# Three sums of magnitudes instead of eight, three whole products and a new order, in a two-level seven-product matmul

## The chip, the cores and the metric

The kernel runs on one core of a Trainium2 chip. The metric is the device time of one execution in microseconds (us); lower is better. The core's engines are PE (matmuls; PEld is its weight loads), DVE and ACT (vector and scalar work), POOL (a second, slower vector engine) and SP (here only the queue that issues DMAs). Each engine works through its own queue in order.

## The reference

```python
B, S, D = 8, 2048, 2048          # x: [B, S, D], w: [D, D], float32
cs = np.cumsum(x, axis=1)
diff = cs - shifted(cs)          # shifted by one row: diff is x again
return np.matmul(diff, w)
```

So what must be computed is x @ w: 16384 rows, 2048 by 2048 weights.

## The kernel before, in words

The 128 row tiles of x (128 rows each) are worked in two ways. The first four ("plain") are multiplied directly while the weights arrive: per half h of the output columns and per 128 rows ko of the weights, `plain.h.r.ko` is two matmuls for row tile r. x reaches the kernel in quarters there (`first x.q.r`, 256 KB each), which DVE casts (`cast x`), PE transposes (`turn x`) and an engine copies out of PSUM (`turned x`). Weights come as 512 KB pieces (`w.h.ko`), cast to 16 bits by ACT (`cast w`).

The other 124 tiles go in 31 groups of four, numbered 0 to 30 (`period[0]`; `PERIOD` is one group in the order table). A group's four tiles g, h, k, l are a 2 by 2 block matrix, multiplied by seven products P1 to P7 instead of eight (Strassen's scheme in Winograd's form). P6 is done whole. Each of the other six is itself done by seven quarter products instead of eight (class `Seven`): a quarter product is four matmuls of 128x512. For these the weights of each product exist as sums too: of the quarters t11, t12, t21, t22 of a block, Q2 and Q3 (and for most Q4) are made once by DVE (`quarters`, `make`; Q2 overwrites t12's place) and Q1, Q3 or Q4 that aren't kept are made anew in each group into one buffer, `flow` (`ask`). T1 to T4 are sums of weight blocks, made once at the start. `Seven.slot(i)` records the sums of x that a quarter product needs on DVE (`s1` to `s4`), the matmuls (`P3.0` to `P3.6`), copies between PSUM banks or to a lent buffer on ACT (`first`, `out2`, `out4`), an addition on DVE (`middle`) and, after it, one on POOL (`last`). Results are put together in C11, C12, C21, C22 by ACT (`keep`), DVE and POOL, and SP writes them out (`put`).

x of the groups comes by `load` (512 KB) into one of three buffers of F, is cast by ACT (`narrow`), summed in magnitude by ACT as a check of its range (`weigh`), and turned by a DMA (`turn`); the next `load` into that buffer waits for `turn` and `weigh`. `see` is a like check on results: ACT sums the magnitudes of a whole C (128x1024), and its unneeded output goes into the spare half of the F buffer that was loaded last, so a later `load` into that buffer waits for it as well. All checks meet in `judge` (`flag1` to `flag9`, one 1x1 matmul, `vote`); if it finds a fault, the whole product is done again in a slow way, which doesn't happen with these inputs.

Nothing here is scheduled by the order of the code: every operation is recorded with a label, and `emit` sorts all of them by `places`, a table of numbers by label with rows for groups 0, 1, 2, 28, 29, 30 and one (`None`) for all others. Each engine's queue is its share of that sorted list. Every POOL operation also waits for the last DVE operation ahead of it in the list.

Of the kernel before, what the change touches and what calls it, by code (L numbers as in the profile page):

```python
# [10 lines left out]
def kernel(  # L11
# [6 lines left out]
    nc = tc.nc  # L18
# [12 lines left out]
    ALU = mybir.AluOpType  # L31
# [17 lines left out]
    const = ctx.enter_context(tc.tile_pool(name="const", bufs=1))  # L49
    Wall = const.tile([P, KH, 4 * NH], f32, name="W")  # L50
# [7 lines left out]
    seen_c = tiny[:, 8:16]  # L58
# [309 lines left out]
    class Right:  # L368
# [26 lines left out]
        def ask(self, name):  # L395
            if name in self.s:
                return self.s[name]
            p, q, op = {
                "Q1": ("t22", "Q2", SUB),
                "Q3": ("Q2", "t11", SUB),  # L400
                "Q4": ("t21", "Q2", SUB),
            }[name]
            tensor(f"{self.name}.{name}", flow, self.s[p], self.s[q], op)
            return flow
# [22 lines left out]
    in_3.quarters(early[3])  # L427
    in_7.quarters(late[0], late[1])
# [7 lines left out]
    for some, to in zip((in_3, in_5, in_1, in_2), late[3:]):  # L436
        some.make("Q4", "t21", "Q2", SUB, to)

# [23 lines left out]
    class Seven:  # L462
        def __init__(self, name, g, h, side, right, to, room, lent):
            self.name = name
            self.a11, self.a12 = (piece(g, side, n) for n in range(2))
            self.a21, self.a22 = (piece(h, side, n) for n in range(2))
            self.right = right
            (self.g0, self.g1), (self.h0, self.h1) = to
            self.r1, self.r2 = room or (self.a21, self.a11)
            self.r4 = self.r2 if room else self.a12  # L470
            self.lent = lent
# [3 lines left out]

        def slot(self, i):
            n = self.name
# [29 lines left out]
    def see(c, i):  # L507
        if period[0] == 1:
# [4 lines left out]
                lambda: nc.scalar.activation(other, c, ABS, accum_out=seen_c[:, i : i + 1]),  # L513
# [52 lines left out]
    def group(g, xy, zv):  # L566
        h, k, l = g + 1, g + 2, g + 3
# [3 lines left out]
        def ready(t, i):  # L571
            nonlocal ready_last
            ready_last = t, i
# [50 lines left out]
        for u, v, p, s, t in ((C21g, C22g, zv[0], "g", g), (C21h, C22h, zv[1], "h", h)):  # L624
            c = free.pop(0)
            for i in range(2):
                tensor(f"C12{s}.{i}", c[:, i, :], p[i], v[:, i, :], ADD)
                if s == "h" and i == 1:
                    plus("P3.last", c[:, i, :], lz, "pool")
# [12 lines left out]
        for c, v, p, s in ((C21g, C22g, xy[0], "g"), (C21h, C22h, xy[1], "h")):  # L642
            for i in range(2):
                plus(f"C21{s}+P7.{i}", c[:, i, :], p[i])
                if s == "h" and i == 1:
# [53 lines left out]
    def judge():  # L699
# [4 lines left out]
        dve("flag4", lambda: ins.tensor_scalar(flags[:, 8:16], seen_c, FINITE, None, ALU.is_le))  # L704
        dve("flag5", lambda: ins.tensor_reduce(flags[:, 1:2], flags[:, 8:16], AX.X, ALU.min))
# [36 lines left out]
            'first x.0.0': -710913, 'cast w.0.0': -708588, 'numbers turned': -640017,  # L742
            'eye': -620640, 'first x.0.1': -615478, 'first x.2.3': -611089,
# [517 lines left out]
```

## Time and profile before

| | us |
|---|---|
| median of 3 runs | 1457.49 (1455.3 to 1457.54) |
| profiled execution, its own time | 1456.21 |
| its span in the trace | 1454.3 |
| PE busy | 1424.5, 98% of the span |
| DVE / ACT / POOL busy | 1302.5 / 1046.1 / 552.1 |

The profiled execution's time is 1.9 us more than its span, and 1.3 us less than the median. PE is busy nearly always, so the time is PE's work plus the gaps in it; the gaps are few, and they lie at the start, in the first groups and in the last. Groups 3 to 27 take 43.6 us each.

### The profile page before, as it was taken

To read this page: it belongs to the slowest core of one execution; us is meant where nothing else is said; L and a number is where in the kernel's file an instruction comes from. 1 tells how busy PE (TensorE), PEld (TensorE's weight loads), DVE (VectorE), ACT (ScalarE), POOL (GpSimd) and SP (SyncE) were. 2 spreads that over 40 slices of the span, in tenths; PEclk is the share of its full clock that TensorE was granted. 3 is DMA by queue.
4 is the path that set the end of the run, shared out by engine and by line. 5 is a ranking of instruction groups with operands and counts; after the bars stand their busy time and mean duration, and the time that the engine had idled before them with its cause. 6 is when DMAs were issued, how large, how long until landed. Compare 5 with 4: busy or idle time off the path is not lost. (4 is left out here: it accounts for less than half of the span.)

```text
span 1454.3 us, 20618 instructions
## 1 busy us (share of the span) xinstructions
PE 1424.5 (98%) x6543; PEld 630.1 (43%) x6543; DVE 1302.5 (90%) x2107; ACT 1046.1 (72%) x1716; POOL 552.1 (38%) x376
## 2 busy tenths in 40 slices
PE   8999899999999999999999999999999999999997
PEld 3443334444444444444444444444444444444443
DVE  2799879999999999999999999999999999999997
ACT  5877867777777767777777777777777777776773
POOL 0014423444433444433444433444433444433444
PEclk9999999999999999999999999999999999999999
DMA  9998698888888898788888888898888898888883
GB/s 362 350 259 217 188 231 237 250 249 229 240 243 239 247 249 230 239 241 240 247 250 229 242 236 244 247 254 225 246 238 240 252 253 222 247 239 226 252 223 121
DMA packets 343792, 351.64 MB, mean 242 GB/s; under 512 B 270976, under 2 KB 270976, under 8 KB 343680
## 3 DMA queue, kind: packets, MB, share of 16 engines
q1 hardware_dynamic: 343680, 350.29, 84.3%
q8 instruction: 52, 0.85, 0.2%
q14 instruction: 60, 0.49, 0.1%
HBM read 150.99 MB, written 134.22 MB: 196 GB/s over the span
## 5 line engine op out<-in xcount | busy, mean ns | idle before, releaser
L126 POOL TENSOR_TENSOR arena<-arena 128x512 f32<-128x512 f32 x372 | 551.9, 1491 | 896.8 <-DVE arena L126 623.7
L129 ACT COPY arena<-b 128x512 f32<-128x512 f32 x729 | 407.2, 588 | 257.6 <-PE b L450 127.7
L450 PE MATMUL b<-W,x 128*128 128x512 f16 x2108 | 521.2, 379 | 2.1 <-DVE x L126 1.0
L450 PEld LDWEIGHTS <-x 128*128 128x128 f16 x3224 | 314.5, 98 | 396.4 <-issue 21.9
L126 DVE TENSOR_TENSOR arena<-W 128x2048 f16<-128x2048 f16 (+1 forms) x287 | 367.6, 1281 | 23.5 <-PE b L450 23.4
L450 PE MATMUL b<-W,arena 128*128 128x512 f16 x1364 | 344.0, 379 | 5.8 <-DVE arena L126 3.8
L450 PEld LDWEIGHTS <-arena 128*128 128x128 f16 x1984 | 189.1, 98 | 254.8 <-DVE arena L126 35.9
L129 ACT CAST F<-F 128x1024 f16<-128x1024 f32 x248 | 260.2, 1049 | 44.5 <-DMA F<-in_x_dram 40.6
L450 PE MATMUL b<-arena,x 128*128 128x512 f16 x1116 | 281.6, 379 | 4.4 <-ACT arena L129 4.4
L163 ACT ACTIVATE F<-F 128x1024 f16<-128x1024 f16 x248 | 263.1, 1062 | 1.1
L126 DVE TENSOR_TENSOR arena<-arena,b 128x512 f32<-128x512 f32 x372 | 247.7, 678 | 11.1 <-PE b L450 9.6
L543 PE MATMUL b<-W,x 128*128 128x512 f16 x992 | 250.1, 381 | 1.6 <-DVE x L126 1.6
L126 DVE TENSOR_TENSOR x<-x,x 128x1024 f16<-128x1024 f16 (+1 forms) x372 | 232.8, 633 | 6.2 <-DMA x<-F 3.8
L129 ACT COPY b<-b 128x512 f32<-128x512 f32 x186 | 107.3, 577 | 78.0 <-DVE arena L126 62.0
L450 PE MATMUL b<-arena 128*128 128x512 f16 x620 | 159.1, 379 | 2.3 <-DVE arena L126 2.1
L126 DVE TENSOR_TENSOR b<-b,arena 128x512 f32<-128x512 f32 x217 | 150.1, 692 | 11.4 <-ACT arena L129 11.0
L543 PEld LDWEIGHTS <-x 128*128 128x128 f16 x992 | 95.3, 98 | 122.3 <-DVE x L126 12.0
L126 DVE TENSOR_TENSOR arena<-b,arena 128x512 f32<-128x512 f32 x155 | 105.3, 681 | 18.5 <-PE b L450 17.0
L126 DVE TENSOR_TENSOR arena<-x,x 128x512 f16<-128x512 f16 x124 | 56.8, 458 | 31.9 <-PE b L450 31.7
L126 DVE TENSOR_TENSOR arena<-x 128x512 f16<-128x512 f16 x124 | 59.3, 479 | 1.2 <-PE b L450 0.2
L126 DVE TENSOR_TENSOR x<-x 128x512 f16<-128x512 f16 x124 | 56.6, 457 | 3.3 <-PE b L450 1.5
L126 DVE TENSOR_TENSOR arena<-arena,x 128x512 f16<-128x512 f16 x124 | 54.2, 437 | 2.6
(43 smaller groups left out, 301.4 us busy)
## 6 DMA issues: line engine op xcount, KB each, us to landing
F<-in_x_dram SPq DMA_DIRECT2D x248, 512.0 KB, 5.0
out_dram<-arena SPq DMA_DIRECT2D x240, 512.0 KB, 3.7
W<-in_w_dram SPq DMA_DIRECT2D x32, 512.0 KB, 9.0
out_dram<-arena SPq DMA_DIRECT2D x32, 256.0 KB, 3.4
W<-in_x_dram SPq DMA_DIRECT2D x16, 256.0 KB, 7.0
x<-F SPq DMA_TRANSPOSE x248, 3.2
```

What stands on the lines that cost most here:

```text
L126: record(label, engine, lambda: on.tensor_tensor(dst, p, q, op))
L129: record(label, "act", lambda: nc.scalar.copy(to, p))
L163: return nc.scalar.activation(other, data, ABS, accum_out=m)
L450: said = nc.tensor.matmul(to, a[:, ds(k * P, P)], b[:, k, :], start=(start and k == 0), stop=(k == 3), skip_group_check=True,)
L543: said = nc.tensor.matmul(to[n], half(t, 0)[:, k, :], T2[k][:, n, :], start=False, stop=(k == KH - 1), skip_group_check=True,)
```

## The change

It has four parts.

1. `see`: instead of all eight C of group 1, three are summed: `see.3` (C21h) of group 29, `see.1` (C11h) and `see.5` (C12h) of group 30. `flag4` and `flag5` work on three columns.
2. P3 and P7 in group 0 and P7 in group 30 are done whole, by eight quarter products (`w0` to `w7`) without sums of x or of weights. In group 30 the quarter t12 of in_7's block, which Q2 has overwritten by then, is made again (`in7.t12`).
3. The sums of quarters for in_3 and in_7 (six, `in3.make` and `in7.make`) are recorded in group 1 rather than in group 0.
4. All rows of `places` have new numbers.

```diff
+    FROM3, FROM7 = 1, 1
+    LAST = (END - PLAIN) // 4 - 1
...
-    seen_c = tiny[:, 8:16]
+    seen_c = tiny[:, 8:11]
...
+                "t12": ("t22", "Q3", SUB),
...
-    in_3.quarters(early[3])
-    in_7.quarters(late[0], late[1])
...
+    def by_quarters():
+        if period[0] == FROM7:
+            in_7.quarters(late[0], late[1])
+        if period[0] == FROM3:
+            in_3.quarters(early[3])
+            in_3.make("Q4", "t21", "Q2", SUB, late[3])
...
+            self.whole = (name == "P3" and period[0] < FROM3) or (
+                name == "P7" and (period[0] < FROM7 or period[0] == LAST)
+            )
...
+        def slot_whole(self, i):
+            pairs = [
+                (to, a, b, start)
+                for to, p, q, c in (
+                    (self.g0, self.a11, self.a12, 1),
+                    (self.g1, self.a11, self.a12, 2),
+                    (self.h0, self.a21, self.a22, 1),
+                    (self.h1, self.a21, self.a22, 2),
+                )
+                for a, b, start in ((p, f"t1{c}", True), (q, f"t2{c}", False))
+            ]
+            for j in (0, 1) if i == 0 else (i + 1,):
...
+                quarter(f"{self.name}.w{j}", to, a, self.asked[b], start)
...
     def see(c, i):
-        if period[0] == 1:
+        rows = {1: LAST, 5: LAST, 3: LAST - 1}
+        if i in rows and period[0] == rows[i]:
...
     def group(g, xy, zv):
+        by_quarters()
...
-                if s == "h" and i == 1:
+                if s == "h" and i == 1 and not P3.whole:
                     plus("P3.last", c[:, i, :], lz, "pool")
...
-            'P1.0': -29977, 'P1.s1': -20682, 'P1.s2': -16636, 'P1.first': -15550, 'P1.2': -15057,
+            'P1.0': -30279, 'P1.s1': -22233, 'P1.first': -16350, 'P1.s2': -16053, 'P1.2': -15126,
```

What the new numbers do to the queues is seen at three places.

**DVE, group 0, from the `middle` of P5 on, before** (b are PSUM banks, x the turned tiles, W the weight blocks, arena everything else). The rows are in turn P5.middle, in3.Q1, in4.make Q2, S3g, in7.make Q2, P3.s2, keep C22h.1, S3h, in3.make Q4, P3.middle, P3.s4 and C12g.0:

```order
L126 TENSOR_TENSOR b7_81<-b5_79,arena_70 128x512
L126 TENSOR_TENSOR arena_70<-W_58 128x2048
L126 TENSOR_TENSOR W_58<-arena_70,W_58 128x4x512
L126 TENSOR_TENSOR x20_66<-x21_67,x00_62 128x1024
L126 TENSOR_TENSOR W_58<-arena_70,W_58 128x4x512
L126 TENSOR_TENSOR x01_63<-x11_65,x01_63 128x512
L126 TENSOR_TENSOR arena_70<-b5_79,arena_70 128x512
L126 TENSOR_TENSOR x30_68<-x31_69,x10_64 128x1024
L126 TENSOR_TENSOR arena_70<-W_58 128x2048
L126 TENSOR_TENSOR b5_79<-b7_81,arena_70 128x512
L126 TENSOR_TENSOR x01_63<-x01_63 128x512
L126 TENSOR_TENSOR arena_70<-b4_78,arena_70 128x512
```

The same stretch now, from P5.middle: S3g, T3.7, keep C22h.1, S4h, in4.make Q2, in4.Q1, C12g.1, S3h, C12g.0, P4.s1 and then the first two of the moved sums, in3.make Q2 and in7.make Q3 of group 1:

```order
L128 TENSOR_TENSOR x20_66<-x21_67,x00_62 128x1024
L128 TENSOR_TENSOR W_58<-W_58 128x2x512
L128 TENSOR_TENSOR arena_70<-b5_79,arena_70 128x512
L128 TENSOR_TENSOR x11_65<-x11_65,x10_64 128x1024
L128 TENSOR_TENSOR W_58<-arena_70,W_58 128x4x512
L128 TENSOR_TENSOR arena_70<-W_58 128x2048
L128 TENSOR_TENSOR arena_70<-b5_79,arena_70 128x512
L128 TENSOR_TENSOR x30_68<-x31_69,x10_64 128x1024
L128 TENSOR_TENSOR arena_70<-b4_78,arena_70 128x512
L128 TENSOR_TENSOR x31_69<-x31_69 128x512
L128 TENSOR_TENSOR W_58<-W_58 128x4x512
L128 TENSOR_TENSOR arena_70<-W_58 128x2048
```

The sums for P3 are gone from between, and these two moved sums stand behind C12g.0, which uses P3's result. Of the other four, in3.make Q3 stands far ahead, before the first sum of x in group 0; in7.make Q2 and in3.make Q4 stand just ahead of P4.s4 of group 0, and in7.make Q4 inside group 1.

**ACT, where group 1 ends and group 2 begins, before.** The rows are P1.out2 of group 2, three `see` of group 1, P1.out4, P2.first, keep C11g.0 and .1, narrow7.0, P2.out2, narrow6.0 and keep C11h.0 (narrow and see belong to group 1):

```order
L129 COPY arena<-b_76 128x512
L513 ACTIVATE F,tiny<-arena 128x1024 x3
L129 COPY arena<-b_76 128x512
L129 COPY b_78<-b_80 128x512
L129 COPY arena<-b_74 128x512
L129 COPY arena<-b_75 128x512
L129 CAST F<-F 128x1024
L129 COPY arena<-b_80 128x512
L129 CAST F<-F 128x1024
L129 COPY arena<-b_76 128x512
```

Now no `see` stands there, and narrow6.0 (the first row) comes ahead of P1.out2, followed by narrow7.1, P1.out4, P2.first, keep C11g.1 and .0, and narrow7.0:

```order
L131 CAST F<-F 128x1024
L131 COPY arena<-b_76 128x512
L131 CAST F<-F 128x1024
L131 COPY arena<-b_76 128x512
L131 COPY b_78<-b_80 128x512
L131 COPY arena<-b_75 128x512
L131 COPY arena<-b_74 128x512
L131 CAST F<-F 128x1024
```

**ACT, where group 29 ends and group 30 begins, now.** The rows are P1.first of group 30, weigh5.1 and weigh6.1 of group 29, see.3, P1.out2, P2.first, P1.out4, narrow6.0 of group 29, keep C11g.0, narrow7.1 and P2.out2:

```order
L131 COPY b_74<-b_76 128x512
L165 ACTIVATE F,told<-F 128x1024 x2
L546 ACTIVATE F,tiny<-arena 128x1024
L131 COPY arena<-b_76 128x512
L131 COPY b_78<-b_80 128x512
L131 COPY arena<-b_76 128x512
L131 CAST F<-F 128x1024
L131 COPY arena<-b_74 128x512
L131 CAST F<-F 128x1024
L131 COPY arena<-b_80 128x512
```

Here a `see` has come in: see.3 stands behind P1.first, and in SP's queue load6.0 of group 29 stands behind it (its buffer is the one that see.3 writes to). Before, load6.0 of group 29 came ahead of P1.first of group 30.

More of the change, by code (lines that the diff above doesn't have):

```diff
@@ L435 @@
     in_4.make("Q2", "Q3", "t11", ADD, in_4.s.pop("t12"))
-    for some, to in zip((in_3, in_5, in_1, in_2), late[3:]):
+    for some, to in zip((in_5, in_1, in_2), late[4:]):
         some.make("Q4", "t21", "Q2", SUB, to)
+    def by_quarters():
[4 more added lines that the diff above has]
+            in_3.make("Q4", "t21", "Q2", SUB, late[3])
     room = [rooms_at[:, j, :] for j in range(2)]
@@ L467, in __init__ @@
             self.right = right
+            self.whole = (name == "P3" and period[0] < FROM3) or (
+                name == "P7" and (period[0] < FROM7 or period[0] == LAST)
+            )
+            self.asked = {}
             (self.g0, self.g1), (self.h0, self.h1) = to
@@ L474, in sum @@
             tensor(f"{self.name}.s{n}", to, p, q, op, engine)
+        def slot_whole(self, i):
[10 more added lines that the diff above has]
+            for j in (0, 1) if i == 0 else (i + 1,):
+                to, a, b, start = pairs[j]
+                if b not in self.asked:
+                    self.asked[b] = self.right.ask(b)
+                quarter(f"{self.name}.w{j}", to, a, self.asked[b], start)
         def slot(self, i):
+            if self.whole:
+                return self.slot_whole(i)
             n = self.name
@@ L512, in see @@
                 "act",
-                lambda: nc.scalar.activation(other, c, ABS, accum_out=seen_c[:, i : i + 1]),
+                lambda: nc.scalar.activation(other, c, ABS, accum_out=seen_c[:, i // 2 : i // 2 + 1]),
             )
@@ L572, in ready @@
             nonlocal ready_last
-            ready_last = t, i
+            if t < END:
+                ready_last = t, i
             load(t, i)
@@ L644, in group @@
                 plus(f"C21{s}+P7.{i}", c[:, i, :], p[i])
-                if s == "h" and i == 1:
+                if s == "h" and i == 1 and not P7.whole:
                     plus("P7.last", c[:, i, :], lx, "pool")
@@ L703, in judge @@
         dve("flag3", lambda: ins.tensor_reduce(flags[:, 0:1], fits, AX.XY, ALU.min))
-        dve("flag4", lambda: ins.tensor_scalar(flags[:, 8:16], seen_c, FINITE, None, ALU.is_le))
-        dve("flag5", lambda: ins.tensor_reduce(flags[:, 1:2], flags[:, 8:16], AX.X, ALU.min))
+        dve("flag4", lambda: ins.tensor_scalar(flags[:, 8:11], seen_c, FINITE, None, ALU.is_le))
+        dve("flag5", lambda: ins.tensor_reduce(flags[:, 1:2], flags[:, 8:11], AX.X, ALU.min))
         dve(
@@ L734 @@
         0: {
[7 rows of a table removed]
-            'first x.0.0': -710913, 'cast w.0.0': -708588, 'numbers turned': -640017,
-            'eye': -620640, 'first x.0.1': -615478, 'first x.2.3': -611089,
[156 rows of a table removed]
-        },
[47 rows of a table removed]
-        },
[46 rows of a table removed]
[6 rows of a table added]
+            'numbers': -1144010, 'first x.0.1': -1046174, 'numbers turned': -988555,
[56 rows of a table added]
+            'cast w.1.4': -249602, 'one': -249513, 'turn0.0': -249053, 'out': -248802,
[96 rows of a table added]
+        },
[48 rows of a table added]
+        },
[45 rows of a table added]
         },
         28: {
[44 rows of a table removed]
[44 rows of a table added]
         },
         29: {
[45 rows of a table removed]
[46 rows of a table added]
         },
         30: {
[43 rows of a table removed]
[42 rows of a table added]
         },
         None: {
[44 rows of a table removed]
[44 rows of a table added]
         },
```

853 rows, old and new, of the table places are left out of this document.

## Prediction

> **What bounds the kernel now.** I read the page first.
>
> ```profile
> span 1454.3 us, 20618 instructions
> PE 1424.5 (98%) x6543; PEld 630.1 (43%) x6543; DVE 1302.5 (90%) x2107; ACT 1046.1 (72%) x1716; POOL 552.1 (38%) x376
> ```
>
> PE is the bound, so time can come only from fewer matmuls or from the 30 us in which PE stands. To place those, I cut the span where a group's first product starts (from the timeline of PE); the columns are length, busy time of PE, PEld, DVE, ACT and POOL, granted clock, DMA share and GB/s.
>
> ```profile
> 0.00:10.42 10.42, 7.63 (x23) 2.73 (x23) 2.96 (x9) 3.27 (x3) 0.20 (x4) 1.00 0.80 258
> 10.42:46.02 35.60, 31.93 (x190) 15.77 (x191) 11.44 (x23) 27.09 (x30) 0.00 (x0) 1.00 1.03 406
> ...
> 72.36:119.63 47.27, 44.17 (x202) 19.16 (x201) 45.80 (x66) 34.94 (x60) 10.48 (x7) 1.00 0.92 252
> 119.63:165.80 46.17, 42.72 (x193) 18.31 (x192) 41.30 (x65) 35.73 (x60) 16.21 (x12) 1.00 0.73 205
> 165.80:214.65 48.85, 43.66 (x189) 18.46 (x188) 39.01 (x61) 35.12 (x61) 12.73 (x10) 0.97 0.85 217
> 214.65:1305.05 1090.40, 1089.48 (x5001) 483.13 (x5000) 1003.39 (x1625) 797.93 (x1326) 445.60 (x301) 1.00 0.85 241
> 1305.05:1397.85 92.80, 91.72 (x421) 40.66 (x420) 87.01 (x139) 65.31 (x109) 41.34 (x27) 1.00 0.87 235
> 1397.85:1447.12 49.27, 46.80 (x210) 19.93 (x208) 45.95 (x78) 24.54 (x42) 23.55 (x17) 1.00 0.49 155
> 1447.12:1454.29 7.17, 0.00 (x0) 0.00 (x0) 0.98 (x2) 0.00 (x0) 2.02 (x2) 0.74 0.54 191
> ```
>
> The rows are: the start in two pieces, groups 0, 1 and 2, groups 3 to 27, 28 and 29, 30, and the tail. Groups 3 to 27 have 0.9 us of idle PE in 1090.40: nothing is left there, and their 1090.40/5001 = 0.218 us is the price of a matmul. Groups 0, 1 and 2 have 3.1, 3.4 and 5.2 us, group 30 has 2.5, the tail 7.2. DVE is busy for 45.80 of group 0's 47.27 us: there it is DVE that paces. Whom PE waits for in those groups, from its timeline (start, length, and in brackets the idle time before and who ended it):
>
> ```profile
> 76.05 1.02 PE L450 MATMUL b<-W,arena 128*128 128x512 f16 x4 [1.37 <-ACT b L129]
> 103.86 1.04 PE L450 MATMUL b<-W,x 128*128 128x512 f16 x4 [0.51 <-DVE x L126]
> 114.41 1.04 PE L450 MATMUL b<-arena 128*128 128x512 f16 x4 [0.88 <-DVE arena L126]
> ...
> 128.00 1.90 PE L450 MATMUL b<-W,arena 128*128 128x512 f16 x8 [1.90 <-DVE arena L126]
> 149.24 1.89 PE L450 MATMUL b<-W,x 128*128 128x512 f16 x8 [0.77 <-ACT b L129]
> ...
> 175.35 1.90 PE L450 MATMUL b<-W,arena 128*128 128x512 f16 x8 [0.72 <-DVE arena L126]
> 185.94 1.02 PE L450 MATMUL b<-arena,x 128*128 128x512 f16 x4 [2.34 <-ACT arena L129]
> 187.37 3.40 PE L543 MATMUL b<-W,x 128*128 128x512 f16 x8 [0.40 <-DVE x L126]
> ```
>
> The last row is eight matmuls in 3.40 us, twice their usual time. The clock by stretches says why:
>
> ```profile
> 187.61:191.02 3.41, 3.41 (x10) 1.21 (x9) 3.38 (x7) 1.87 (x5) 0.00 (x0) 0.50 0.99 303
> 184.20:187.61 3.41, 1.26 (x6) 0.41 (x6) 1.68 (x4) 3.25 (x6) 0.00 (x0) 1.00 0.76 182
> ```
>
> After 3.41 us in which PE was busy for 1.26, the clock was granted by half for the next 3.41 us: 1.7 us lost on top of the waits. The Trainium skill ("TensorE: Matmul & The Clock Gate", Part 1) tells of windows of this length, but halves the clock after an idle one; here a wait of 2.34 us was enough.
>
> **Part 1, the sums of C.** The wait of 2.34 us is for a copy on ACT (P2.out4), and its chain is read on ACT and SP:
>
> ```profile
> 175.89 1.06 ACT L513 ACTIVATE F<-arena 128x1024 f16<-128x1024 f32 x1
> ...
> 183.61 1.04 ACT L129 CAST F<-F 128x1024 f16<-128x1024 f32 x1 [2.90 <-issue]
> 184.82 1.07 ACT L129 COPY arena<-b 128x512 f32<-128x512 f32 x2 [0.16 <-DMA out_dram<-arena]
> ```
>
> ```profile
> 177.07 0.33 SPq L145 DMA_DIRECT2D F<-in_x_dram  x1
> ```
>
> see.3 ends at 177.0, and at 177.07 the load goes out that needs the F buffer see.3 wrote to; narrow6.0 waits for it until 183.61, and the copy P2.out4 stands behind narrow6.0. Without the `see` of group 1 that load waits only for weigh5.1. So the 2.34 goes, and with it the half clock; eight sums also leave ACT in groups 1 and 2:
>
> ```profile
> L513 ACT ACTIVATE F<-arena 128x1024 f16<-128x1024 f32 x8 | 8.4, 1056 | 0.5 <-POOL arena L126 0.3
> L513 ACT ACTIVATION_READ_ACCUMULATOR F<-arena 128x1 f32 x8 | 1.5, 188 | 0.0
> ```
>
> That is 9.9 us of ACT. The same chain is built anew in group 30: see.3 of group 29 waits for POOL's P4.last, load6.0 for see.3, narrow6.0 for the load, and P2.out2 stands behind narrow6.0, with P2.4 behind that. Counted in products from the end of P4.6 of group 29 (0): see.3 runs from about 1.1 to 2.4 (POOL has three operations of 1.49 to do behind P7.6, which ends 3.5 us before), the load lands 5.0 later, at 7.4, then come narrow6.0 (1.05), keep C11g.0 (0.6), narrow7.1 (1.05) and P2.out2 (0.6): 10.7. P2.4 is due nine products of 0.87 after P4.6 and a short wait, at 8.1. That is a wait of 2.6, an estimate from the two rows below; with a load faster or slower by 1 it is 1.6 to 3.6. I take 2.4.
>
> ```profile
> F<-in_x_dram SPq DMA_DIRECT2D x248, 512.0 KB, 5.0
> L126 POOL TENSOR_TENSOR arena<-arena 128x512 f32<-128x512 f32 x372 | 551.9, 1491 | 896.8 <-DVE arena L126 623.7
> ```
>
> see.1 and see.5 stand 1 us or more ahead of the next need of ACT's copies: nothing.
>
> **Part 2, whole products.** Three products of eight quarter products: 3 x 4 matmuls x 0.218 = +2.6 us, all on PE. What goes is DVE work:
>
> ```profile
> L126 DVE TENSOR_TENSOR arena<-W 128x2048 f16<-128x2048 f16 x283 | 366.0, 1293 | 23.5 <-PE b L450 23.4
> L126 DVE TENSOR_TENSOR x<-x 128x512 f16<-128x512 f16 x124 | 56.6, 457 | 3.3 <-PE b L450 1.5
> L126 DVE TENSOR_TENSOR b<-b,arena 128x512 f32<-128x512 f32 x217 | 150.1, 692 | 11.4 <-ACT arena L129 11.0
> ```
>
> In group 0: two Q1 (2.6), eight sums of x (3.7), two `middle` (1.4), 7.7 us in all; in group 30 about 2.5 net of in7.t12. Of the waits of group 0, the 0.51 and 0.88 were for sums (P3.s4, P7.s3) that no longer exist, and the 1.37 was for P1.first, which now has two more pieces of plain work (four matmuls, 0.9 us) to be done in before P1.2. That could be 2.8 of 3.1; I leave 1.0 for what remains and for new waits: **-2.1**.
>
> **Part 3, the moved sums.** Six of 1.29, but five still run within group 0's time, so group 1 gets only 1.3 us more; with part 2, DVE reaches group 1 with some 7.7 + 1.3 us less behind it. The 1.90 before P1.4 (for P1.s3, in DVE's backlog), the 0.72 of group 2 and smaller ones go, and the 0.77 (ACT) with the `see`: group 1 keeps 1.0 of 3.4, **-2.4**; group 2 keeps 0.7 of 5.2 and loses the half clock, -4.5 - 1.7 = **-6.2**. These bounds are 0 and -3.4, 0 and -6.9.
>
> **Part 4, the order.** At the start, landing follows the order of issue (406 GB/s: 0.65 us for a quarter of x). The first transpose waits for DVE's cast:
>
> ```profile
> 9.67 0.69 DVE L217 CAST W<-W 128x1024 f16<-128x1024 f32 x1 [6.39 <-DMA W<-in_x_dram]
> ...
> 10.42 0.62 PE L226 MATMUL b<-arena,W 128*128 128x128 f16 x8 [1.60 <-DVE W L217]
> 12.43 0.62 PE L226 MATMUL b<-arena,W 128*128 128x128 f16 x8 [1.39 <-DVE W L217]
> ```
>
> It was behind five issues, 1.75 MB, and is now behind seven, 2.25 MB: 1.2 us later. But the stretch to 46.02 has 3.7 us of idle PE, and the new order asks for x and weights nearly as they land; between +1.2 and -2, I take **-0.5**. Groups 3 to 27 keep nearly the same order, with some neighbours exchanged: **0**. Groups 28 and 29: **-0.5** of 1.1. Group 30: +2.4 from above; P4.s4 now stands behind C21g+P4.0 and C21h+P4.1, which wait for P4.3, so P4.5 waits about 1.0; of the present 2.5 idle I let 2.3 go (the larger ones are for copies that now have a product more to be done in): **+1.1**. The tail: PE's last product ends at 1447.12, and then
>
> ```profile
> 1446.73 0.69 DVE L126 TENSOR_TENSOR arena<-arena,b 128x512 f32<-128x512 f32 x1 [0.54 <-POOL arena L126]
> 1447.95 0.69 DVE L126 TENSOR_TENSOR arena<-arena,b 128x512 f32<-128x512 f32 x1 [0.53 <-POOL arena L126]
> ```
>
> DVE's last sum waits for POOL, and P4.last and its `put` follow. Now PE does P4.1 early and P7.last is gone, so both are done ahead: the last sum starts 0.8 us sooner and its `put` is the last DMA: **-1.2**.
>
> Sum: 2.6 - 0.5 - 2.1 - 2.4 - 6.2 - 0.5 + 1.1 - 1.2 = -9.2 us. Against the profiled execution's own 1456.21 that is 1447.0, which I also set against the median of 1457.49, 1.3 us above it.
>
> **The rivals.**
>
> *The order of the middle groups stalls (slower).* 25 groups repeat one order with little margin:
>
> ```profile
> 1016.42 1.04 ACT L129 CAST F<-F 128x1024 f16<-128x1024 f32 x1 [1.85 <-DMA F<-in_x_dram]
> 1017.51 1.11 ACT L129 COPY arena<-b 128x512 f32<-128x512 f32 x2
> ```
>
> ```profile
> 1018.79 0.39 PE L450 MATMUL b<-W,arena 128*128 128x512 f16 x1
> ```
>
> narrow7.0 waits for its load, and the second copy (P2.out2) ends at 1018.62, 0.17 us before P2.4 starts; the new order has narrow4.0 ahead of P5.out2 in the same way. 0.37 us per group eats the gain; at 0.6 it costs 15: 1462. Against it: loads are issued in nearly the same places, load4.0 earlier. Chance 0.07, and 0.07 for a half of it, which ends near no change.
>
> *DVE's relief is lost at the start.* w.1.5, which T1.5 needs, was issued right behind w.1.1 and is now the eighth behind it, seven pieces of 1.29 us (512 KB at 406 GB/s) or 9 us later, while T1.5 stays the third of the T1 in DVE's queue. Part of that is covered by T1.5 having waited less before; DVE may stand some 4 us there. Then groups 0 and 1 keep their waits: -9.2 + 4.5, 1451.5. Chance 0.15.
>
> *The clock halves elsewhere.* PE now stands 1.2 us longer before its first transposes, and about 2.4 us in group 30, as long as the wait that halved it in group 2. One stretch costs 1.7, with 1.3 more wait in group 30: 1450. Chance 0.10. By the rule of the Trainium skill quoted above neither would halve the clock, and this rival would end at 1448.3.
>
> *All waits go.* The start gives 2.0, groups 0 and 1 another 2, group 30 the 2.4: 1441. Chance 0.15.
>
> **Numbers.** The sum holds with 0.46. A measurement tells 0.2%, 2.9 us, from no change: faster is below 1454.6, which all but the first rival reach: 0.86; same 0.07; slower 0.07. Range 1440.0 to 1454.0: from all waits gone to the relief lost with one more halving.
>
> **What would show it.** In the profile after: 6555 matmuls; no wait over 1 us and no half clock in groups 1 and 2; 133 us from the first product of group 0 to that of group 3 (142.29 before, + 1.7 - 10.7); 43.6 per group in the middle; a wait of some 2 us in group 30 ended by an ACT copy behind a cast that waited for a load. A middle of 43.9 or more per group would prove the sum wrong, as would waits for DVE in group 1.

## The result, and the profile after

The changed kernel takes 1467.99 us (median of 6 runs, 1466.34 to 1469.17), the kernel before 1457.33 beside it: a ratio of 1.0072 (95% interval 1.0059 to 1.0085). It is 10.7 us slower, where 10.5 us less were forecast. First the head of the page after:

```profile
span 1466.3 us, 20642 instructions
PE 1426.2 (97%) x6555; PEld 632.0 (43%) x6555; DVE 1360.5 (93%) x2090; ACT 1025.3 (70%) x1697; POOL 565.5 (39%) x373
```

PE does 12 matmuls more, as said, and ACT has 21 us less. But DVE, which has 17 instructions fewer, is busy 58 us longer. The stretches show where the time went (cut as before: the start up to the first transpose and in two pieces more, groups 0, 1, 2, then 3 to 27, 28 and 29, 30, and the tail; columns as in the prediction):

```profile
0.00:11.91 11.91, 6.97 (x22) 2.57 (x22) 3.01 (x10) 3.27 (x3) 0.20 (x4) 1.00 0.83 275
11.91:46.02 34.11, 33.55 (x197) 17.18 (x198) 9.02 (x17) 27.93 (x32) 0.00 (x0) 0.95 1.03 405
46.02:70.32 24.30, 23.20 (x108) 10.37 (x107) 18.48 (x36) 19.08 (x24) 0.00 (x0) 1.00 1.08 325
70.32:119.47 49.15, 46.83 (x214) 20.70 (x214) 45.01 (x68) 35.91 (x61) 6.40 (x5) 1.00 0.93 252
119.47:160.62 41.15, 40.56 (x185) 17.42 (x184) 39.84 (x62) 27.85 (x46) 12.68 (x9) 1.00 0.92 234
160.62:204.89 44.27, 43.16 (x197) 18.94 (x196) 41.55 (x64) 31.52 (x52) 17.15 (x13) 1.00 0.91 233
204.89:1317.08 1112.19, 1092.45 (x5005) 484.15 (x5004) 1069.38 (x1626) 788.59 (x1328) 467.00 (x302) 1.00 0.85 237
1317.08:1406.38 89.30, 87.95 (x402) 38.45 (x400) 84.51 (x132) 61.58 (x103) 34.96 (x25) 1.00 0.81 228
1406.38:1461.24 54.86, 51.23 (x233) 22.14 (x231) 48.86 (x79) 29.56 (x53) 26.94 (x19) 1.00 0.58 172
1461.24:1466.30 5.06, 0.28 (x2) 0.08 (x1) 0.81 (x3) 0.00 (x0) 0.22 (x1) 0.66 0.56 191
```

Group 3 begins at 204.89 instead of 214.65: 9.8 us ahead. From group 28 to the end it is 149.22 us, 149.24 before. All that was lost, 21.8 us, lies in groups 3 to 27: 1112.19 us instead of 1090.40, 44.5 per group instead of 43.6, in groups whose matmuls are the same as before. PE's waits for DVE's results (total, number, longest):

```profile
PE b L459 <- DVE arena L128: 22.6, 30, 1.0
```

25 of the 30 lie one in each of groups 4 to 28, always at the same place: before P1.1, which needs in1.Q1 (DVE, 128x2048). Before, at the boundary of groups 20 and 21, the rows of DVE, POOL and PE were these (the first row of DVE holds C21g+P4.0 and C21h+P7.0, that of POOL C22h+C21.0 and P7.last):

```profile
1005.00 1.27 DVE L126 TENSOR_TENSOR arena<-arena,b 128x512 f32<-128x512 f32 x2
...
1007.62 1.22 DVE L126 TENSOR_TENSOR arena<-W 128x2048 f16<-128x2048 f16 x1 [0.42 <-PE b L450]
...
1006.35 3.63 POOL L126 TENSOR_TENSOR arena<-arena 128x512 f32<-128x512 f32 x2
...
1008.29 1.03 PE L450 MATMUL b<-W,x 128*128 128x512 f16 x4
1009.15 1.03 PE L450 MATMUL b<-arena 128*128 128x512 f16 x4
```

And after, at the same boundary:

```profile
1011.77 1.27 DVE L128 TENSOR_TENSOR arena<-arena,b 128x512 f32<-128x512 f32 x2
1012.97 2.33 DVE L128 TENSOR_TENSOR arena<-W 128x2048 f16<-128x2048 f16 x1
...
1011.53 2.69 POOL L128 TENSOR_TENSOR arena<-arena 128x512 f32<-128x512 f32 x2
...
1013.51 1.03 PE L459 MATMUL b<-W,x 128*128 128x512 f16 x4
1015.35 1.02 PE L459 MATMUL b<-arena 128*128 128x512 f16 x4 [0.81 <-DVE arena L128]
```

The same two pieces of work have changed roles. Before, in1.Q1 took 1.22 us and POOL's pair 3.63; after, in1.Q1 takes 2.33 and POOL's pair 2.69. Split into single records, P7.last began at 1007.70 before, 0.08 us behind in1.Q1, and took 2.28; after, it begins at 1012.95, 0.02 us ahead of in1.Q1, and takes 1.27. Who starts first runs at full speed, the other waits it out, about 1.1 us. POOL can afford that; DVE can't, since P1.1 waits: from the start of P1.3 to that of P1.1 it is 1.84 us instead of 0.86, 0.98 more. (The 0.81 of the row is counted from the modelled end of P1.3.) The 1.1 us, 25 times, are also 28 of the 58 us by which DVE is busy longer. The rest costs PE nothing that shows: in the kernel with P7.last moved, further down, DVE is busy for 1334.4 us, 32 more than before, and the middle groups are as fast as before.

What tipped it is one changed place on DVE. Before, C21g+P4.0 stood ahead of C21h+P7.0. In the first of the rows after (x2: C21h+P7.1 and C21g+P4.0) it stands between C21h+P7.1 and in1.Q1, so in1.Q1 starts 0.16 us behind the end of P4.6, which releases its buffer, and not 0.03. P7.last starts 0.14 behind that end (0.11 before).

The Trainium skill ("SBUF — State Buffer", "Who interferes with whom") says that a DVE instruction with two inputs in SBUF contends with a GpSimd (here POOL) instruction that reads SBUF: "Issue order, not op shape, decides who blocks." By the same page of the Trainium skill ("SBUF: two separate sides") whichever of the two starts first has the shared pair of ports for its whole length, and the other is blocked. The trace agrees: 1.22 and 2.28 in one order, 2.33 and 1.27 in the other. It also agrees that a DVE instruction with only one input in SBUF (the other is in PSUM) is free of this: the two sums of the row of 1011.77 take 0.67 us each while POOL works.

### The profile page after: what moved, and what is told of

Read it like the earlier page. It is cut to its first block, busy times and chain, and to the rows that moved or that the text cites. A ratio compares the mean times of both kernels' runs of the same rounds, so it can differ in the third digit from the quotient of the medians.

```text
span 1466.3 us, 20642 instructions
## 1 busy us (share of the span) xinstructions
PE 1426.2 (97%) x6555; PEld 632.0 (43%) x6555; DVE 1360.5 (93%) x2090; ACT 1025.3 (70%) x1697; POOL 565.5 (39%) x373
## 4 chain that ended last, share of the span: by engine, by line
PE 79%; DVE 11%; DMA 7%; ACT 1%; issue 1%; POOL 1%; SPq 0%; ACTq 0%; DVEq 0%; POOLq 0%
PE b L459 65%; PE b L576 14%; DVE arena L128 10%; DMA F<-in_x_dram 2%; DMA W<-in_x_dram 1%; DMA W<-in_w_dram 1%; DMA x<-F 1%; DMA out_dram<-arena 1%; DVE x L128 1%; POOL arena L128 1%; ACT F L131 0%; ACT arena L131 0%; DVE b L128 0%; ACT W L131 0%; SPq L213 0%
## 5 line engine op out<-in xcount | busy, mean ns | idle before, releaser
L128 POOL TENSOR_TENSOR arena<-arena 128x512 f32<-128x512 f32 x369 | 565.3, 1545 | 895.7 <-DVE arena L128 581.7
L459 PEld LDWEIGHTS <-x 128*128 128x128 f16 x3268 | 317.0, 98 | 397.5 <-issue 23.8
L128 DVE TENSOR_TENSOR arena<-W 128x2048 f16<-128x2048 f16 x284 | 377.5, 1330 | 7.7 <-PE b L459 6.0
L459 PE MATMUL b<-W,arena 128*128 128x512 f16 x1348 | 336.7, 379 | 3.1 <-ACT arena L131 1.9
L459 PE MATMUL b<-arena,x 128*128 128x512 f16 x1108 | 275.2, 379 | 0.8 <-ACT arena L131 0.5
L128 DVE TENSOR_TENSOR x<-x,x 128x1024 f16<-128x1024 f16 (+1 forms) x370 | 221.2, 605 | 5.0 <-PE b L459 1.0
L459 PE MATMUL b<-arena 128*128 128x512 f16 x604 | 154.9, 379 | 21.3 <-DVE arena L128 21.3
L128 DVE TENSOR_TENSOR arena<-x 128x512 f16<-128x512 f16 x122 | 93.4, 766 | 1.0
L128 DVE TENSOR_TENSOR arena<-x,arena 128x512 f16<-128x512 f16 x122 | 81.4, 668 | 9.5 <-PE b L459 9.5
L128 DVE TENSOR_TENSOR arena<-arena,x 128x512 f16<-128x512 f16 x122 | 64.2, 526 | 1.2
L266 PE MATMUL b<-W,arena 128*128 128x512 f16 x240 | 55.0, 382 | 1.5 <-ACT W L131 1.5
```

What stands on the lines that cost most here:

```text
L128: record(label, engine, lambda: on.tensor_tensor(dst, p, q, op))
L266: said = nc.tensor.matmul(to[n], xP[:, r, ko, :], b[:, n, :], start=(ko == 0), stop=(ko == KO - 1))
L459: said = nc.tensor.matmul(to, a[:, ds(k * P, P)], b[:, k, :], start=(start and k == 0), stop=(k == 3), skip_group_check=True,)
```

## Experiments: the middle groups

Ratios are to runs of the kernel before on the same chip, with 95% intervals.

**C21g+P4.0 behind in1.Q1.** Its number in the row of groups 3 to 27 (this takes it out of the way of in1.Q1, but to the other side of where it stood before the change; its old place, ahead of C21h+P7.0, was not tried alone):

```diff
-            'P4.6': 84587, 'P7.last': 84656, 'put1.1': 85522, 'C21g+P4.0': 86531,
+            'P4.6': 84587, 'P7.last': 84656, 'put1.1': 85522, 'C21g+P4.0': 86700,
```

> The changed kernel with one place of the middle groups altered: C21g+P4.0 (DVE) stands behind in1.Q1 instead of ahead of it. Theory (DVE and POOL take turns; who starts second waits): in the changed kernel in1.Q1 starts 0.16 us after the end of P4.6 and 0.02 us after POOL's P7.last, and takes 2.33 us instead of 1.22; with the exchange it starts some 0.03 us after P4.6, ahead of P7.last, takes 1.2, P7.last 2.3, and the wait of about 0.97 us before P1.1 goes from groups 4 to 28: 24 us less, about 1444 to 1447. Rival one (the wait comes from another exchange, of PE's products or ACT's casts): the wait stays, 1468. Rival two (only the 0.13 us by which in1.Q1 starts later matters): about 3 us less, 1465.

Measured: 1453.65 us, ratio 0.9965 (0.9952 to 0.9977).

```profile
1004.65 1.23 DVE L128 TENSOR_TENSOR arena<-W 128x2048 f16<-128x2048 f16 x1 [0.41 <-PE b L459]
...
1003.32 3.69 POOL L128 TENSOR_TENSOR arena<-arena 128x512 f32<-128x512 f32 x2
...
1008.39 0.82 PE L459 MATMUL b<-W,arena 128*128 128x512 f16 x3 [0.33 <-DVE arena L128]
```

in1.Q1 is first again, at 1.23 us, POOL pays, and P1.1 doesn't wait. But three sums now stand behind in1.Q1 and ahead of P1.s4 and P1.s3, so that P1.4 waits for those, and from one boundary to the next it is mostly 43.85 us (43.50 in the kernel before; the 43.6 above is the mean of the stretch). So both rivals are out, but 14.3 us came back where 24 were expected. The profiled run also lost 3 us in group 0, where the clock was granted by half (last section).

**DVE's order left, POOL's turn moved.** P7.last of the middle groups is put behind in1.Q1 in the list, and so waits for it:

```diff
+    places[None]['P7.last'] = 86700
```

> The changed kernel with P7.last (POOL) of the middle groups placed behind in1.Q1 in the order, so that it waits for in1.Q1; DVE's order is as in the changed kernel, with C21g+P4.0 ahead of in1.Q1. Theory (taking turns): in1.Q1 starts as late as in the changed kernel (0.16 us after P4.6) but takes 1.2 us, so P1.1 doesn't wait: 1444 to 1448, if POOL's 1.2 us of lateness harms nothing. Rival (the wait is DVE's order alone, C21g+P4.0 ahead): in1.Q1 stays at 2.3 us and the time at 1468.

Measured: 1444.67 us, ratio 0.9911 (0.9895 to 0.9928).

```profile
996.72 1.21 DVE L128 TENSOR_TENSOR arena<-W 128x2048 f16<-128x2048 f16 x1
...
998.06 1.27 POOL L128 TENSOR_TENSOR arena<-arena 128x512 f32<-128x512 f32 x1 [1.33 <-ACT F L131]
```

The stretch of groups 3 to 27 in this kernel:

```profile
203.43:1294.18 1090.75, 1090.00 (x5006) 484.21 (x5005) 1045.44 (x1626) 790.77 (x1328) 468.40 (x302) 1.00 0.88 242
```

in1.Q1 starts as late as in the changed kernel (0.16 us behind P4.6), yet takes 1.21 us; the middle groups take 1090.75 us, with 0.75 idle. One number takes 23.3 us off the changed kernel, the whole loss, and leaves it 13 us under the kernel before.

**The fault put into the kernel before.** C21g+P4.0 placed directly ahead of in1.Q1 there:

```diff
+    places[None]['C21g+P4.0'] = 84700
```

> The kernel before with one place of its middle groups altered: C21g+P4.0 (DVE) put directly ahead of in1.Q1, as in the changed kernel. Theory (taking turns): in1.Q1 starts level with or behind POOL's P7.last (0.08 us ahead of it now), takes 2.3 us, and P1.1 waits for 0.9 to 1.0 us in groups 4 to 28: 1478 to 1482. If C21g+P4.0 finds room ahead of P4.6's end, so that in1.Q1 keeps its 0.08 us, nothing changes: 1457. Rival (another exchange): 1457.

Measured: 1481.50 us, ratio 1.0157 (1.0140 to 1.0174): 23.8 us more by the medians.

```profile
1024.97 2.31 DVE L126 TENSOR_TENSOR arena<-W 128x2048 f16<-128x2048 f16 x1
...
1023.52 2.68 POOL L126 TENSOR_TENSOR arena<-arena 128x512 f32<-128x512 f32 x2
...
1027.34 1.02 PE L450 MATMUL b<-arena 128*128 128x512 f16 x4 [0.68 <-DVE arena L126]
```

The roles and the price are those of the changed kernel, but the tie was turned from the other side. in1.Q1 starts 0.03 us behind the end of P4.6, no later than before; it is P7.last that comes sooner, 0.01 us ahead of that end instead of 0.11 behind it, because the POOL sum that it follows directly starts 0.18 us sooner. Why that sum does was not asked.

**And healed there.** The same kernel, with P7.last behind in1.Q1. (At the last of these boundaries P7.last then comes behind a copy of group 28 that overwrites its operand, so C21 of group 27 holds other numbers.)

```diff
+    places[None]['C21g+P4.0'] = 84700
+    places[None]['P7.last'] = 85100
```

> The kernel before with C21g+P4.0 ahead of in1.Q1 (which cost 24 us: 1481.5), and now P7.last (POOL) behind in1.Q1. Theory (taking turns): in1.Q1 is back at 1.2 us, groups at 43.5, 1457 to 1458. Rival (C21g+P4.0 ahead of in1.Q1 costs by itself): 1470 to 1481.

Measured: 1460.86 us, ratio 1.0021 (1.0011 to 1.0031). in1.Q1 takes 1.22 us again and, by the ratios, 20 of 23 us are back; from boundary to boundary it is mostly 43.67 us instead of 43.50. So the turn explains most of it. As for the little that stays: P1.s4 starts as long behind the end of P4.6 as before (2.38 us), but beside P7.last, which now runs there, it takes 0.57 us instead of 0.42. That speaks for the new place of P7.last and against a cost of C21g+P4.0 by itself; no run parts the two.

**The old row of numbers for groups 3 to 27 in the changed kernel.**

> The changed kernel with the numbers of the middle groups (3 to 27) of the kernel before, all else as changed. Theory: the loss of about 24 us is in the order of the middle groups alone, the rest of the forecast holds: 43.5 us per group, 1444 to 1448. Rival (the loss comes from something else of the change that lasts, as the state in which groups 0 to 2 leave the queues): about 1468.

Measured: 1460.28 us, ratio 1.0015 (1.0005 to 1.0024). Inside, groups mostly take 43.5 us, as the theory has it; but at the seams, where this row meets the new rows of groups 2 and 28, about 7.5 and 3.7 us are lost:

```profile
205.99:257.37 51.38, 45.20 (x202) 19.12 (x201) 42.49 (x64) 31.76 (x54) 16.26 (x12) 1.00 0.76 205
257.37:1308.61 1051.24, 1048.14 (x4802) 463.47 (x4800) 966.06 (x1561) 765.27 (x1273) 426.49 (x288) 1.00 0.87 240
1308.61:1361.66 53.05, 49.68 (x225) 21.60 (x224) 46.33 (x75) 35.01 (x58) 21.03 (x16) 1.00 0.86 214
```

A row of an order can't be swapped alone; its time was a miss for that reason.

## Experiments: groups 0 to 2

The forecast had group 3 begin 9.5 us sooner (0.5 from the start, 9.0 from these groups), and 9.8 came. The next runs ask whether for the reasons given.

**The eight sums of magnitudes left out, and one of them moved**, both in the kernel before:

```diff
-        if period[0] == 1:
+        if period[0] == -1:
```

> The kernel before without the eight sums of magnitudes of C (that check is left out; flag4 looks at the sum over the weights instead), order unchanged. Theory (the prediction's): the load that waited for see.3 goes out earlier, the 2.34 us wait and the half clock of group 2 go, and smaller waits for ACT: 4 to 6 us less, 1451.5 to 1453.5; group 2 from its first product to that of group 3 takes 43 to 45 us instead of 48.85. Rival (the waits of groups 1 and 2 come from DVE's backlog, which the sums don't touch, and a wait for ACT is replaced by one for DVE): 1 us or less, 1456.5.

Measured: 1455.10 us, ratio 0.9980 (0.9970 to 0.9991): 2.9 us, less than the theory and more than the rival.

```diff
+    places[1]['see.3'] = 212030
```

> The kernel before, all eight sums kept, but see.3 of group 1 placed behind weigh7.0, 12 us later in ACT's queue, so that load6.0 doesn't wait for it. Theory: that one place carries the 2.34 us wait and the half clock behind it, 4.0 us: 1453 to 1454. Rival (the work of the eight sums on ACT counts, 9.9 us, not the place of one): at most 1 us, 1456.5.

Measured: 1456.94 us, ratio 0.9991 (0.9981 to 1.0000): 1.3 us, near the rival. The number put see.3 further back than was meant: in the trace it runs at 232.47, 57 us later and not 12. For load6.0 of group 1 that is the same; what it costs further on is in the time, too. In both traces the half clock of group 2 is gone, but little else; without the eight sums, the stretch of group 2 (48.85 us before), and then ACT and PE in it:

```profile
166.23:213.40 47.17, 41.84 (x190) 18.03 (x189) 39.61 (x61) 30.20 (x50) 12.73 (x10) 1.00 0.84 225
```

```profile
181.07 1.04 ACT L129 CAST F<-F 128x1024 f16<-128x1024 f32 x1 [2.16 <-DMA F<-in_x_dram]
...
182.66 1.89 PE L450 MATMUL b<-W,arena 128*128 128x512 f16 x8 [1.45 <-ACT arena L129]
...
186.95 1.25 PE L543 MATMUL b<-W,x 128*128 128x512 f16 x5 [1.23 <-DVE x L126]
```

The 2.34 us in front of P2.6 is down to 0.15, and 1.45 and 1.23 us have come up before P2.4 (P2.out2, behind narrow7.0, which waits for its own load) and P6h.0.0. So the half clock is won, and of the wait nothing is. One trace alone wouldn't show the first, since with the eight sums in place the half clock comes in some executions only (last section). But the mean granted clock of the runs, 0.9973 without the sums and 0.9962 in the kernel before on the same chip, says the same: 0.0011 of 1455 us is 1.6 us, and one half stretch costs 1.7.

**DVE's six sums left out**, in the kernel before (and the eight of ACT with them):

```diff
-    in_3.quarters(early[3])
-    in_7.quarters(late[0], late[1])
+    for odd in (in_3, in_7):
+        odd.s.update(Q2=odd.s.pop("t12"), Q3=odd.s["t22"], Q4=odd.s["t21"])
...
-    for some, to in zip((in_3, in_5, in_1, in_2), late[3:]):
+    for some, to in zip((in_5, in_1, in_2), late[4:]):
```

> The kernel before without the six sums of weight quarters for in_3 and in_7 (7.7 us of DVE in groups 0 and 1, at 1.29 each); P3 and P7 then use weights as they lie, so the numbers of the result are others, with the same instructions otherwise. The eight sums of magnitudes stay. Theory (DVE's backlog makes the waits of 1.04, 2.06, 0.34, 0.63 in groups 0 and 1): these go, and some of group 2's; group 3 begins 4 to 6 us earlier, 1452 to 1454. Rival (the waits have other causes, the magnitudes alone): 1 us or less, 1456.5.

Measured: 1457.95 us, ratio 0.9996 (0.9986 to 1.0006): nothing. (The trace is that of its fastest run, 1454.07 us, and has group 0 1.6 us shorter; the median of ten doesn't show it.)

> The kernel before without the six sums of weight quarters and without the eight sums of magnitudes. Theory (two causes, which hide each other in group 2: ACT's chain behind see.3, and DVE's backlog): the two gains add up or more, 7 to 9 us, 1449 to 1451, and group 2 takes 43.5 to 45 us. Rival (one of the two is enough): no better than the better of the two alone.

Measured: 1453.87 us, ratio 0.9965 (0.9951 to 0.9979): 4.0 us by the medians where 7 to 9 were expected, 1.4 more than leaving out the eight sums alone brings (the intervals of the two overlap), nearer to the rival. Without 7.7 us of DVE's work the wait before P1.4 of group 1 stands as it did (first row, without the six sums). With the six sums in place and P1.s3 put directly behind P1.s4 it shrinks (second row):

```profile
127.27 1.04 PE L450 MATMUL b<-W,arena 128*128 128x512 f16 x4 [1.90 <-DVE arena L126]
```

```profile
127.69 1.04 PE L450 MATMUL b<-W,arena 128*128 128x512 f16 x4 [0.70 <-DVE arena L126]
```

That second kernel:

```diff
+    places[1]['P1.s3'] = places[1]['P1.s4'] + 1
```

> The kernel before with one place of group 1 altered: P1.s3 on DVE directly behind P1.s4, ahead of C21h+P4.1 and P1.middle, as it stands in the changed kernel. Theory (the waits of groups 1 and 2 are made by the order close by, not by a backlog): P1.s3 ends about 1.3 us earlier and the wait of 2.06 us before P1.4 in group 1 becomes 0.7 to 1.0; 1456.5. Rival (backlog: the wait is moved, not shortened): 2 us stay in front of P1.4 or the next product, 1457.9.

Measured: 1456.47 us, ratio 0.9986 (0.9977 to 0.9996). The wait was no backlog. It was made by two sums between P1.s4 and P1.s3, and by P1.s4 itself, which beside a sum of POOL takes 1.53 us in the first of these traces. The gain is about 2 us (0.6 to 3.4 by the ratio), the size of the wait at best: part of it comes up again before later products of groups 1 and 2.

**The six sums left out of the changed kernel** (with P7.last moved):

> The changed kernel with P7.last behind in1.Q1 in the middle groups (1444.7), without the six sums of weight quarters for in_3 and in_7, so that P3 and P7 use weights as they lie (other numbers in the result, the same instructions otherwise). Theory (DVE has room there now, and had none to give before): 1 us or less, 1444. Rival (DVE's backlog is still the bound of groups 0 to 2): 2 to 4 us less, 1441 to 1442.5.

Measured: 1446.72 us, ratio 0.9920 (0.9897 to 0.9944), against 0.9911 with them: nothing again. In the profiled runs groups 0 to 2 together take 133.45 us without the sums and 133.31 with them. So DVE's load is not what bounds these groups in either kernel, as far as intervals of 1.5 and 3.5 us to each side can tell.

## Experiments: the last group

**see.3 later.** Group 30 in the changed kernel shows the chain that was forecast: see.3 and narrow6.0 with the copy P2.out2 behind it on ACT, the load in SP's queue, and P2.4:

```profile
1415.39 1.06 ACT L546 ACTIVATE F<-arena 128x1024 f16<-128x1024 f32 x1 [0.45 <-POOL arena L128]
...
1422.06 1.04 ACT L131 CAST F<-F 128x1024 f16<-128x1024 f32 x1 [2.16 <-DMA F<-in_x_dram]
...
1416.57 0.81 SPq L147 DMA_DIRECT2D F<-in_x_dram  x2
...
1425.07 1.24 PE L459 MATMUL b<-W,arena 128*128 128x512 f16 x5 [1.40 <-ACT arena L131]
```

```diff
+    places[None]['P7.last'] = 86700
+    places[29]['see.3'] = 261660
```

> The changed kernel with P7.last behind in1.Q1 in the middle groups (1444.7 in the run before), and see.3 of group 29 placed behind weigh7.1, 17 us later in ACT's queue. Theory: load6.0 then goes out when weigh5.1 is done, 2 to 3 us earlier, narrow6.0 doesn't hold up P2.out2, and the wait of 1.6 us before P2.4 in group 30 goes: 1442.5 to 1443.5. Rival (the bank's copy is late for another cause, narrow7.1 or keep C11g.0 ahead of it): 1444.5.

Measured: 1443.94 us, ratio 0.9911 (0.9895 to 0.9928), the shortest median of all, though its interval is that of the kernel with P7.last alone moved. P2.4 still waits:

```profile
1399.66 0.59 PE L459 MATMUL b<-W,arena 128*128 128x512 f16 x2 [0.70 <-ACT arena L131]
```

Half of the wait was see.3's. Here P2.out2 starts 0.07 us after P2.1 has ended, so the other half can be that P2.4 follows P2.1 directly; but narrow7.1, ahead of P2.out2 on ACT, ends at the same moment, and this trace doesn't part the two.

**DVE's sums ahead of POOL's at the start of group 30**, in addition:

```diff
+    places[29]['C21h+P4.0'] = 190350
+    places[29]['P4.last'] = 190360
+    places[29]['C22g+C21.1'] = 190400
```

> As the kernel with see.3 later, and at the start of group 30 in1.Q1, P1.s4 and P1.s3 stand ahead of C21h+P4.0 on DVE, and ahead of P4.last and C22g+C21.1 on POOL, so that these three sums don't run beside POOL's. Theory (taking turns): in1.Q1 takes 1.2 us instead of 1.38, P1.s4 0.4 instead of 1.48, and the waits before P1.1 (0.47) and P1.4 (0.89) go: 1.0 to 1.4 us less than the kernel with see.3 alone moved, 1441 to 1442.5. Rival (the banks that C21h+P4.0 empties are needed at once): PE waits there instead, no gain or a loss of up to 1 us.

Measured: 1446.42 us, ratio 0.9926 (0.9910 to 0.9943): 2.5 us more by the medians than without, though the intervals overlap. DVE with see.3 later, then with this:

```profile
1390.36 1.37 DVE L128 TENSOR_TENSOR arena<-W 128x2048 f16<-128x2048 f16 x1
1391.65 1.48 DVE L128 TENSOR_TENSOR arena<-x,arena 128x512 f16<-128x512 f16 x1
```

```profile
1391.69 1.23 DVE L128 TENSOR_TENSOR arena<-W 128x2048 f16<-128x2048 f16 x1 [0.19 <-PE b L459]
1392.84 0.42 DVE L128 TENSOR_TENSOR arena<-x,arena 128x512 f16<-128x512 f16 x1
1394.28 0.43 DVE L128 TENSOR_TENSOR arena<-x,x 128x512 f16<-128x512 f16 x1 [1.03 <-PE b L459]
...
1395.82 1.98 DVE L128 TENSOR_TENSOR arena<-W 128x2048 f16<-128x2048 f16 x1
1397.72 1.48 DVE L128 TENSOR_TENSOR arena<-x 128x512 f16<-128x512 f16 x1
```

in1.Q1 and P1.s4 run at full speed as expected; but P1.s3 has to wait for PE anyway, and POOL's two sums, now later, hold up in1.Q4 (1.98 us) and P2.s1 (1.48) instead. Both theories missed: the blocking was moved to other sums, and nothing was won.

**P4.s4 earlier**, on the kernel with see.3 later:

```diff
+    places[30]['P4.s4'] = places[30]['C21g+P4.0'] - 1
```

> The kernel with P7.last behind in1.Q1 and see.3 later (1443.9), and P4.s4 of group 30 placed ahead of C21g+P4.0 on DVE. Theory (the prediction's: P4.5 waits because P4.s4 stands behind C21g+P4.0 and C21h+P4.1): the wait of 0.69 before P4.5 goes, and the end comes 0.4 to 0.7 us earlier, 1443.3. Rival (the end hangs on the sums that are now later by 0.5, so nothing is won): 1443.9.

Measured: 1445.08 us, ratio 0.9906 (0.9889 to 0.9922), against 0.9911 (0.9895 to 0.9928) without: a gain as small as the one expected can't be told by these times. PE at P4.5, before and with this:

```profile
1434.97 1.04 PE L459 MATMUL b<-W,x 128*128 128x512 f16 x4 [0.52 <-DVE x L128]
```

```profile
1437.13 1.03 PE L459 MATMUL b<-W,x 128*128 128x512 f16 x4
```

The wait before P4.5 is gone, and yet the end comes 7.8 us after the start of P4.6 (1436.27) instead of 7.4 (1433.42). In these two runs the end hangs on the last sums and their DMAs, as the rival had it: POOL's last sum ends 0.2 us later, counted from P4.6.

## Why the prediction was wrong

- **Groups 3 to 27, "nearly the same order, with some neighbours exchanged: 0"** is the step that failed: 21.8 us instead of 0, and with it the sign: 44.5 us per group, where the prediction itself named 43.9 as the sign that its sum is wrong. The term was put at nothing without pricing the exchanged neighbours; one of them made in1.Q1 start second to P7.last, and it then took 2.33 us instead of 1.22 in 25 groups. With that turn alone set right (P7.last moved) the change takes 1444.67 us, inside the range. The first rival, a stall in the middle groups, had the effect and about the size (0.98 us at P1.1, 0.87 net per group, where 0.37 and 0.6 were priced), but sought its cause in ACT's queue, and gave it a chance of 0.07. The trace of before had the sign: a POOL sum of 2.28 us beside a mean of 1.49, beginning 0.08 us behind a DVE sum that PE needs next. Each changed place next to it could turn the two round, and had to be priced as a rival at 25 times 1 us.
- **Start, -0.5**: -2.0 (first product of group 0 at 70.32, not 72.36). The first transpose came 1.5 us later, where 1.2 was reckoned, and the clock was granted at 0.95 in the next stretch (one half stretch, 1.7 us); more was won behind it.
- **Group 0, +1.7 - 2.1**: +1.9 us (49.15 instead of 47.27). PE is busy 2.7 us longer, the whole products with it, and idle 0.8 less, not 2.1: the waits named in the prediction are gone, but P6g.1.0 now waits 1.9.
- **Groups 1 and 2, -2.4 and -6.2**: -5.0 and -4.6 us. The sum was right, its reasons were not, so that was luck. A wait that had DVE as its releaser was read as DVE's backlog; leaving out 7.7 us of DVE's work gained nothing, and placing one sum otherwise shortened the wait. The `see` chain was real and brought the half clock (1.7 us) with it in some executions, but the 2.34 us wait was covered by others just behind it. Which of the new places brings the rest wasn't taken apart.
- **Group 30, +1.1, and groups 28 and 29, -0.5**: together PE's idle time grew by 1.4 us (1.35 and 3.63, where it was 1.08 and 2.47). The chain behind see.3 came as drawn, load and all, at 1.40 us instead of 2.4; P4.5 waits for P4.s4, 0.53 instead of 1.0.
- **Tail, -1.2**: -2.3 us. PE's last product ends at 1461.43, 0.2 us inside the last row of the table, so the tail is 4.9 us, not 7.2.

## What to carry to other kernels

Where DVE and POOL start within a tenth of a microsecond of each other, on operands that all lie in SBUF, the earlier start decides who stands (here 1.1 us each time); in a loop body that is a price per round, and it belongs into the estimate of any reordering, however small. Make the order explicit there (let POOL wait for the DVE instruction that is on the path). And before a wait is put down to an engine's load, take the load away: if the wait stays, look at the order next to it.

## What was not expected of the hardware

A difference of 0.1 us in one start moved 1.1 us from one engine to another in each of 25 groups, the same way every time (P7.last took 2.25 to 2.28 us at these places before, 1.26 to 1.27 after).

And the length of a wait doesn't tell whether the clock is halved. The wait of 2.34 us that the prediction shows was followed by half the clock. So was one of only 1.96 us at the same place in the kernel before with C21g+P4.0 moved; but one of 2.49 us in group 3, in the changed kernel with the old row, was not, nor were waits of 1.95 us and 1.91 us at the place of the 2.34 (without the six sums, and with P1.s3 moved). What tells is a grid. In the traces the granted clock changes only at instants that lie whole multiples of 3.413 us apart: in the kernel before it is full for 180.91 us (53 of them), half for 3.41, full for 1259.52 (369). Two stretches on this grid and what follows each, first from the changed kernel with C21g+P4.0 moved (a wait of 2.54 us in group 0), then with the old row (the wait of 2.49 us, which begins at 222.75 and so lies across an instant of the grid):

```profile
85.75:89.16 3.41, 1.32 (x7) 0.49 (x5) 2.37 (x4) 1.23 (x2) 0.00 (x0) 1.00 1.17 286
89.16:92.57 3.41, 2.96 (x8) 1.01 (x8) 2.00 (x4) 2.91 (x6) 0.00 (x0) 0.50 1.00 270
```

```profile
223.27:226.68 3.41, 1.44 (x7) 0.70 (x8) 2.88 (x4) 0.00 (x0) 0.00 (x0) 1.00 1.26 312
226.68:230.09 3.41, 2.19 (x11) 0.88 (x9) 3.41 (x6) 1.08 (x3) 1.31 (x1) 1.00 0.19 41
```

Cut on this grid, the 16 traces of this case have, up to 1430 us, 18 stretches in which the clock was full and PE was busy for at most 1.33 us (14 of them at the start, where PE waits for its first x); each was followed by half the clock. In the 6639 other stretches at full clock PE was busy for 1.44 us or more, and none was. (In the tail of the changed kernel one with 1.54 us was.) So whether a wait of 2 us costs another 1.7 depends on where it falls on the grid, and with the same kernel that can differ from one execution to the next.
